# Feed-forward up projections by pairs of m-tiles, in seven block products of 256 tokens

## The chip, the core and the metric

The kernel runs on one core of a Trainium2 chip. The metric is the device time of one execution in microseconds, from the first instruction to the last and what lies around them. Three runs of the kernel before gave 2783.45, 2782.04 and 2782.11 us, median 2782.11. The profile is of one further execution of 2784.78 us.

## What is computed

Two decoder layers on 512 tokens of width 1024, each with a feed-forward, a mixer (a gated delta rule beside attention) and a second feed-forward:

```python
def swiglu(h, w1, w3, w2):
    return (jax.nn.silu(h @ w1) * (h @ w3)) @ w2

for l in range(DEPTH):
    mod = cond @ ada_w[l] + ada_b[l]                 # nine vectors of 1024: shift, scale, gate, three times
    h = modulate(x, norm_ffn1[l], sh1, sc1)
    x = x + 0.5 * (1.0 + g1)[:, None] * swiglu(h, ffn1_w1[l], ffn1_w3[l], ffn1_w2[l])
    h = modulate(x, norm_mix[l], sh2, sc2)
    y = token_mix(h, ...)
    x = x + (1.0 + g2)[:, None] * y
    h = modulate(x, norm_ffn2[l], sh3, sc3)
    x = x + 0.5 * (1.0 + g3)[:, None] * swiglu(h, ffn2_w1[l], ffn2_w3[l], ffn2_w2[l])
```

Everything is float32. w1 and w3 are 1024 x 2816, w2 is 2816 x 1024. The products concerned are h @ w1 and h @ w3 of the four feed-forwards.

## The kernel before

**Number format.** TensorE takes float32r here. Each operand is split into a high part (a copy rounded to float32r, on ScalarE) and a low part (what is left, a subtraction on VectorE), and a product is three matmuls: high by high, high by low, low by high. `mm3` issues them, the weight part being the stationary operand; the activations h lie in `hhi` and `hlo`, features on the 128 partitions, 8 k-tiles of 512 tokens each.

**A slab.** The weights of one m-tile (128 output features) of w1 or w3 are one transfer of 512 KB into a `raw` buffer (2 of them), issued from SyncE (L117). `slab` makes the high part `whi` and the low part `wlo` (3 buffers each) in two halves of 512 columns (L120, L121).

**Up projection.** `up(m)` loads the slabs of w1 and w3 for m-tile m, multiplies each by all 8 k-tiles of h (24 matmuls of 512 columns into a PSUM bank, tags `acc` and `sc`), and `glu` takes SiLU of the one (L443), multiplies it by the other (L444) and splits the result into high and low (L134, L135), which stay in SBUF for the down projection. There are 22 m-tiles.

**Order within a feed-forward.** m-tiles 0 to 8 up, then `down(0)` over the first eight; 9 to 16 up, `down(1)`; 17 to 21 up, `down(2)`. A down projection (`close`) runs over 8 output tiles with slabs of w2. The last one takes four of its tiles in halves of 256 tokens, with the slabs in `A` buffers, so that the next norm can start on one half. The very first feed-forward has had m-tiles 0 to 2 and half of 3 begun during start-up (`begin`, `first_begun`); the others start with `first`, 256 tokens at a time.

**Work between.** The modulation vectors are computed from 512 KB blocks of ada_w, each a transfer into an `L` buffer (5 of them; the conditioning vector `condb` holds one throughout) and one VectorE operation over 1024 columns (L268), pinned behind whatever was traced on VectorE before it. The blocks wait in `self.queue`; `tick(n)` takes n of them, two per m-tile and one per down tile, and `drain` empties the queue before the mixer. A planner orders each engine's instructions otherwise: it issues what its own clock holds ready, earlier lines first, and a tile's buffer is handed on when its last reader has finished.

The only quoted lines that the functions below do not show are the buffer counts:

```python
BUFS = {
    "raw": 2, "wlo": 3, "whi": 3, "hhi": 1, "hlo": 1, "A": 2, "O": 8, "M": 1, "L": 5, "c3": 5, "cv": 3, "g": 7,
    ...
    "ss": 2, "scl": 2, "rk": 2, "acc": 3, "sm": 2, "sc": 2, "po": 1,
}
```

Of the kernel before, what the change touches and what calls it, by code (L numbers as in the profile page):

```python
# [73 lines left out]
class Trunk:  # L74
# [118 lines left out]
    def setup(self):  # L193
# [5 lines left out]
        self.condb = self.t("L", [P, D])  # L199
# [230 lines left out]

    def ffn(self, l, w, gate, finish, early, ahead=None):

        nc = self.nc
        w1, w3, w2 = (self.ap[f"{w}_{n}"] for n in ("w1", "w3", "w2"))
# [5 lines left out]

        def glu(m, ps1, ps3):
# [3 lines left out]
            third = min(m // 8, 2)  # L445
            if third == 1:
                if m == 8:
                    g["hi"] = self.t("A", [P, KT, SEQ], F32R)
                    g["lo"] = self.t("A", [P, KT, SEQ], F32R)
                hi, lo = g["hi"][:, m - 8, :], g["lo"][:, m - 8, :]  # L450
            else:
                o = self.t("O", [P, 2, SEQ], F32R)
                hi, lo = o[:, 0, :], o[:, 1, :]
            self.split(hi, lo, s)
            g[m] = (hi, lo)

        def up(m):
            s1 = up_slab(w1, m)
            s3 = up_slab(w3, m)
            ps1, ps3 = self.p("acc"), self.p("sc")  # L460
            self.proj(ps1, s1, acts)
            self.proj(ps3, s3, acts)
            glu(m, ps1, ps3)
            if m > 2:
                self.tick(2)
# [15 lines left out]
        def first_begun():  # L481
            n = len(early) // 2
            s = up_slab(w3, n)
            for m in range(n):
                glu(m, early[2 * m], early[2 * m + 1])
            ps = self.p("sc")
            self.proj(ps, s, acts)
            glu(n, early[2 * n], ps)
            return n + 1

        def down(i):
# [817 lines left out]
    def run(self, out):  # L1309
# [12 lines left out]
        for l in range(DEPTH):  # L1322
# [21 lines left out]
            self.condb = self.t("L", [P, D])  # L1344
# [34 lines left out]
def layout(inp):  # L1379
# [77 lines left out]
```

## Time and profile before

| | us |
|---|---|
| median of three runs | 2782.11 (2782.04 to 2783.45) |
| profiled execution, device time | 2784.78 |
| its span, first to last instruction | 2782.7 |
| PE busy | 2745.2 (99%) |
| weight loads busy | 2319.4 (83%) |
| VectorE busy | 1703.3 (61%) |
| ScalarE busy | 1087.0 (39%) |
| Pool busy | 192.6 (7%) |
| mean granted TensorE clock | 0.999 |

The feed-forwards lie at about 28 to 392, 1050 to 1400, 1420 to 1760 and 2430 to 2783 us of the span; 87 SiLU operations of line 443 mark them. In what follows a row of groups reads: line, engine, operation, output and inputs by name, shape, count, then busy time and mean nanoseconds of one, then the idle time before it and what ended that. A row of the timeline reads: start, length, engine, line, operation, shape, count. A row of the windows reads: stretch, its length, busy time of PE, of weight loads, VectorE, ScalarE and Pool with counts, granted clock, DMA share, GB/s.

### The profile page before, as it was taken

Reading aid. Unit: us, or ns where it says so; the run is one execution under the profiler, and the core shown is the slowest. Engines: PE = TensorE matmul, PEld = TensorE weight load, DVE = VectorE, ACT = ScalarE, POOL = GpSimd, SP = SyncE. Lnnn points to the kernel's source line nnn. Section 1 sums busy time; section 2 is a strip of 40 time slices with the busy share of each in tenths; the row PEclk is TensorE's granted clock in tenths of the full one; section 3 lists DMA queues with packets and bytes.
Section 4 is the critical chain, followed back from the end, with each engine's and each line's share of the span. In section 5 each row is a group of like instructions: output and inputs, shape, how many; then the busy total and the mean of one; then the engine's idle time right before and its main releaser. Section 6 shows DMA issues by size and latency. Waiting matters only on the chain. (4 is left out here: it accounts for less than half of the span.)

```text
span 2782.7 us, 38556 instructions
## 1 busy us (share of the span) xinstructions
PE 2745.2 (99%) x14648; PEld 2319.4 (83%) x14648; DVE 1703.3 (61%) x3759; ACT 1087.0 (39%) x2301; POOL 192.6 (7%) x312
## 2 busy tenths in 40 slices
PE   7999999999999999999999999999999999999999
PEld 6888888788888888888888888887888888988888
DVE  6555568767668765543455554787767686653333
ACT  4322245544447433232342222545444564332222
POOL 0000015000001010000000000150000111100000
PEclk9999999999999999999999999999999999999999
DMA  7556433222222343643326563333222223443332
GB/s 280 182 184 203 155 103 114 88 73 80 66 78 74 117 159 121 199 143 99 104 93 197 186 203 116 111 100 95 73 80 73 75 73 117 137 137 98 99 99 91
DMA packets 103720, 339.20 MB, mean 122 GB/s; under 512 B 11760, under 2 KB 14448, under 8 KB 103536
## 3 DMA queue, kind: packets, MB, share of 16 engines
q1 hardware_dynamic: 101088, 332.03, 37.7%
q10 hardware_dynamic: 2448, 4.72, 0.4%
q8 instruction: 115, 1.88, 0.3%
q14 instruction: 69, 0.57, 0.1%
HBM read 321.50 MB, written 15.20 MB: 121 GB/s over the span
## 5 line engine op out<-in xcount | busy, mean ns | idle before, releaser
L120 ACT CAST whi<-raw 128x512 fp32r<-128x512 f32 (+1 forms) x834 | 485.3, 610 | 1090.1 <-issue 519.6
L121 DVE TENSOR_TENSOR wlo<-raw,whi 128x512 fp32r<-128x512 f32 (+1 forms) x834 | 571.0, 706 | 258.3 <-ACT whi L120 251.2
L93 PE MATMUL acc<-hhi,whi 128*128 128x512 f32 (+1 forms) x1648 | 645.2, 392 | 7.5 <-DVE cv L522 5.7
L93 PE MATMUL acc<-hlo,whi 128*128 128x512 f32 (+1 forms) x1648 | 626.2, 380 | 1.1 <-POOL hlo L382 0.3
L93 PE MATMUL acc<-hhi,wlo 128*128 128x512 f32 (+1 forms) x1648 | 625.2, 380 | 0.0
L93 PEld LDWEIGHTS acc<-hhi,whi 128*128 128x128 f32 x1648 | 310.7, 189 | 59.8 <-issue 8.2
L93 PEld LDWEIGHTS acc<-hhi,wlo 128*128 128x128 f32 x1648 | 310.9, 189 | 59.1 <-DVE wlo L1284 0.4
L93 PEld LDWEIGHTS acc<-hlo,whi 128*128 128x128 f32 x1648 | 311.9, 189 | 53.0 <-POOL hlo L382 2.9
L93 PE MATMUL acc<-O,whi 128*128 128x512 f32 x1088 | 336.0, 390 | 0.0
L93 PE MATMUL sc<-hhi,whi 128*128 128x512 f32 (+1 forms) x712 | 272.3, 382 | 0.0
L93 PE MATMUL sc<-hhi,wlo 128*128 128x512 f32 (+1 forms) x712 | 272.2, 382 | 0.0
L93 PE MATMUL sc<-hlo,whi 128*128 128x512 f32 (+1 forms) x712 | 271.9, 382 | 0.0
L93 PEld LDWEIGHTS acc<-O,whi 128*128 128x128 f32 x1088 | 203.5, 188 | 41.7
L444 DVE TENSOR_TENSOR g<-g,sc 128x512 f32<-128x512 f32 x87 | 59.8, 688 | 262.8 <-PE sc L93 259.2
L93 PE MATMUL acc<-O,wlo 128*128 128x512 f32 x544 | 211.9, 390 | 0.0
L388 DVE SCALAR_TENSOR_TENSOR M<-acc,gate,M 128x512 f32<-128x512 f32 (+1 forms) x112 | 77.5, 692 | 198.2 <-PE acc L93 191.8
L93 PE MATMUL acc<-A,whi 128*128 128x512 f32 x640 | 197.1, 389 | 0.0
L268 DVE SCALAR_TENSOR_TENSOR L<-L,L 128x1024 f32<-128x1024 f32 x142 | 169.6, 1220 | 0.0
L93 PEld LDWEIGHTS sc<-hhi,wlo 128*128 128x128 f32 x712 | 133.7, 188 | 27.1 <-DVE wlo L121 1.3
L93 PEld LDWEIGHTS sc<-hhi,whi 128*128 128x128 f32 x712 | 134.1, 188 | 26.0
L93 PEld LDWEIGHTS sc<-hlo,whi 128*128 128x128 f32 x712 | 133.9, 188 | 25.8
L93 PEld LDWEIGHTS acc<-A,whi 128*128 128x128 f32 x640 | 120.1, 188 | 25.0
(370 smaller groups left out, 3674.0 us busy)
## 6 DMA issues: line engine op xcount, KB each, us to landing
raw<-in_ffn_w SPq DMA_DIRECT2D x236, 512.0 KB, 3.6
L<-in_ada_w SPq DMA_DIRECT2D x142, 512.0 KB, 4.6
raw<-in_w_in SPq DMA_DIRECT2D x108, 512.0 KB, 3.5
raw<-in_ffn_w SPq DMA_DIRECT2D x32, 384.0 KB, 3.1
raw<-in_w_branch_a SPq DMA_DIRECT2D x16, 512.0 KB, 3.6
raw<-in_w_branch_b SPq DMA_DIRECT2D x16, 512.0 KB, 3.5
raw<-in_w_out SPq DMA_DIRECT2D x16, 512.0 KB, 3.6
spill<-M SPq DMA_DIRECT2D x16, 256.0 KB, 2.0
```

Source lines behind the costliest of these rows:

```text
L93: i = self.nc.tensor.matmul(*a, **k)
L120: nc.scalar.copy(hi[:, s], raw[:, s])
L121: nc.vector.tensor_sub(lo[:, s], raw[:, s], hi[:, s].bitcast(F32))
L268: self.order(self.nc.vector.scalar_tensor_tensor(raw, raw, 1.0, self.condb, ALU.mult, ALU.mult, accum_out=mod[:, o:o + 1]))
L388: self.nc.vector.scalar_tensor_tensor(self.x[:, m, a:b], ps[:, a:b], gate[:, m:m + 1], self.x[:, m, a:b], ALU.mult, ALU.add)
L444: nc.vector.tensor_mul(s, s, ps3)
```

## The change

Two neighbouring m-tiles of both weights are treated as a 2 by 2 block matrix: rows are m-tiles m and m + 1, columns the two halves of the 1024 input features. h is a 2 by 2 block matrix too: halves of the features by halves of the tokens. The four output blocks are made from seven block products in place of eight, Winograd's form of Strassen's scheme. One block product is, for w1 and w3, four k-tiles in three parts: 24 matmuls of 256 columns into one PSUM bank.

- A host-side layout `w13` stores the weights by m-tile and feature half, w1 and w3 together, one 512 KB block each.
- Per pair, `loads` fetches a11, a12 (into `raw`) and a22, and two sums f1 = a21 + a22 and f3 = a21 + a11 (into `L`), each as a transfer from SyncE followed by an adding transfer issued from Pool. `weights` makes f2 = a11 + f1 and f4 = a12 + f2 in place on VectorE. Each of the seven is split into high and low in one operation of 1024 columns on each of ScalarE and VectorE, up to three ahead (`ahead`).
- `fast_acts` makes the four combinations of h once per feed-forward, in the two `A` buffers: eleven VectorE operations over 1024 columns, four copies on ScalarE, three operations on Pool.
- `pairs` runs the seven products per pair. The bank `x` collects products 0, 2, 4 and 6, and ScalarE copies it out after 0, 2 and 4; `z` collects 1 and 5, `y` holds 3. VectorE and once Pool add what is left; SiLU and the gate product work on 256 tokens at a time.
- m-tiles from 6 on (first feed-forward) or from 4 on (the others) are done in pairs; the groups end at 10, 18 and 22. `tick(2)` comes once per pair, no longer once per m-tile, and already from m = 2 for plain tiles.
- The results of m-tiles 8 and 9 go to `c3`, all others to `O`; `condb` moves from `L` to `kph`.

```diff
-        self.condb = self.t("L", [P, D])
+        self.condb = self.t("kph", [P, D])
...
+    def fast_acts(self):
...
+        f32 = lambda t: t.bitcast(F32)
+        b11, b12, b21, b22 = (quarter(i, j) for i in range(2) for j in range(2))
+        store = [self.t("A", [P, 4, 4, 256], F32R) for _ in range(2)]
+        places = [(st[:, i], st[:, i + 1]) for st in store for i in (0, 2)]
...
+        t = difference(b11, b12, nc.vector)
+        split(places[0], t)
+        t3 = difference(b22, b12, nc.gpsimd)
+        minus_sum(t, b22)
+        split(places[1], t)
+        minus_sum(t, b21)
+        split(places[3], t)
+        split(places[2], t3)
+        return [b11, places[0], places[1], b21, places[2], b22, places[3]]
...
-            if m > 2:
+            if m > 1:
                 self.tick(2)
...
+        def block(tag, m, half):
+            t = self.t(tag, [P, 1024])
+            nc.sync.dma_start(t, w13[l, m, half].rearrange("p w k c -> p (w k c)"))
+            return t
+
+        def block_sum(m, half, m2, half2):
+            t = block("L", m, half)
+            nc.gpsimd.dma_start(t, w13[l, m2, half2].rearrange("p w k c -> p (w k c)"), accum_op=ALU.add)
+            return t
+
+        def loads(m):
+
+            st = {}
+            st["f1"] = block_sum(m + 1, 0, m + 1, 1)
+            yield st
+            st["a11"] = block("raw", m, 0)
+            yield st
+            st["f3"] = block_sum(m + 1, 0, m, 0)
+            yield st
+            st["a12"] = block("raw", m, 1)
+            yield st
+            st["a22"] = block("L", m + 1, 1)
+            yield st
+
+        def weights(st):
+
+
+            def parts(t):
+                hi, lo = self.t("whi", [P, 1024], F32R), self.t("wlo", [P, 1024], F32R)
+                nc.scalar.copy(hi, t)
+                nc.vector.tensor_sub(lo, t, hi[:].bitcast(F32))
+                return hi, lo
+
+            yield parts(st["a11"])
+            yield parts(st["f1"])
+            f2, f4 = st["a11"], st["a12"]
+            nc.vector.tensor_add(f2, f2, st["f1"])
+            yield parts(f2)
+            yield parts(f4)
+            nc.vector.tensor_add(f4, f4, f2)
+            yield parts(st["f3"])
+            yield parts(f4)
+            yield parts(st["a22"])
+
+        def product(ps, f, b, fresh):
+
+            for i in range(2):
+                for k in range(4):
+                    c = slice((4 * i + k) * P, (4 * i + k + 1) * P)
+                    x = (b[0][:, k, :], b[1][:, k, :])
+                    self.mm(ps[:, i, :], f[0][:, c], x[0], start=fresh and i == k == 0, stop=False,
+                            skip_group_check=True)
+                    self.mm(ps[:, i, :], f[0][:, c], x[1], start=False, stop=False, skip_group_check=True)
+                    self.mm(ps[:, i, :], f[1][:, c], x[0], start=False, stop=k == 3, skip_group_check=True)
...
+                for step in range(7):
+                    if step in (2, 3, 4, 5, 6):
+                        got = next(nxt, None)
+                        if step == 3 and got is not None:
+                            forms.append(weights(got))
+                    ahead(3)
+                    f = stream.pop(0)
+                    if step == 0:
+                        x = bank("acc")
+                        product(x, f, comb[0], True)
+                        p1 = half("g")
+                        nc.scalar.copy(p1, x)
+                    elif step == 1:
+                        z = bank("sc")
+                        product(z, f, comb[1], True)
+                        p5 = half("cv")
+                        nc.scalar.copy(p5, z)
+                    elif step == 2:
+                        product(x, f, comb[2], False)
+                        u2 = half("g")
+                        nc.scalar.copy(u2, x)
+                    elif step == 3:
+                        y = bank("sm")
+                        product(y, f, comb[3], True)
+                        nc.vector.tensor_add(p1, p1, y)
+                        gated(p1, 0, HALVES[0], None)
+                    elif step == 4:
+                        product(x, f, comb[4], False)
+                        u3 = half("cv")
+                        nc.scalar.copy(u3, x)
+                        nc.gpsimd.tensor_add(p5, p5, u3)
+                    elif step == 5:
+                        product(z, f, comb[5], False)
+                        nc.vector.tensor_add(u2, u2, z)
+                        gated(u2, 0, HALVES[1], None)
+                        gated(p5, 1, HALVES[1], None)
+                        self.split(*place(m), gm[0])
+                    else:
+                        product(x, f, comb[6], False)
+                        s = self.t("cv", [P, 256])
+                        gated(x, 1, HALVES[0], s)
+                        self.split(*place(m + 1), gm[1])
+                self.tick(2)
...
-        for m in range(first_begun() if len(early) > 3 else first(), 9):
-            up(m)
+        begun = len(early) > 3
+        plain = 6 if begun else 4
+        m = first_begun() if begun else first()
+        comb = None
+        while m < plain:
+            up(m)
+            m += 1
+            if comb is None:
+                comb = self.fast_acts()
+        pairs(range(plain, 10, 2), comb)
         down(0)
-        for m in range(9, 17):
-            up(m)
+        pairs(range(10, 18, 2), comb)
         down(1)
-        for m in range(17, FT):
-            up(m)
+        pairs(range(18, FT, 2), comb)
         down(2)
...
+        out[f"{n}_w13"] = A(np.stack([out[f"{n}_{w}"].reshape(L, FT, P, 2, 4, P) for w in ("w1", "w3")], 4)
+                            .transpose(0, 1, 3, 2, 4, 5, 6))
```

More of the change, by code (lines that the diff above doesn't have):

```diff
@@ L439, in up_slab, with place @@
             return self.slab(src[l, m].rearrange("p k c -> p (k c)"), 1024)
+        def place(m):
+            if m in (8, 9):
+                hi, lo = (self.t("c3", [P, SEQ], F32R) for _ in range(2))
+            else:
+                o = self.t("O", [P, 2, SEQ], F32R)
+                hi, lo = o[:, 0, :], o[:, 1, :]
+            g[m] = (hi, lo)
+            return hi, lo
         def glu(m, ps1, ps3):
@@ L444, in glu @@
             nc.vector.tensor_mul(s, s, ps3)
[L445 to L455, printed above, removed]
+            self.split(*place(m), s)
         def up(m):
@@ L489, in first_begun @@
             return n + 1
+        def block(tag, m, half):
[5 more added lines that the diff above has]
+            nc.gpsimd.dma_start(t, w13[l, m2, half2].rearrange("p w k c -> p (w k c)"), accum_op=ALU.add)
+            return t
+        def loads(m):
[10 more added lines that the diff above has]
+            yield st
@@ new lines, in weights @@
+        def weights(st):
[3 more added lines that the diff above has]
+                nc.vector.tensor_sub(lo, t, hi[:].bitcast(F32))
+                return hi, lo
+            yield parts(st["a11"])
[8 more added lines that the diff above has]
+            yield parts(st["a22"])
@@ new lines, in pairs, with ahead, gated @@
+        def pairs(ms, comb):
+            half = lambda tag: self.t(tag, [P, 2, 256])
+            bank = lambda tag: self.p(tag, [P, 2, 256])
+            stream, steps = [], iter(())
+            def ahead(n):
+                while len(stream) < n and forms:
+                    f = next(forms[0], None)
+                    if f is None:
+                        forms.pop(0)
+                    else:
+                        stream.append(f)
+            forms = []
+            for _ in (lds := loads(ms[0])):
+                st = _
+            forms.append(weights(st))
+            ahead(2)
+            for m in ms:
+                nxt = loads(m + 2) if m + 2 in ms else iter(())
+                x, y, z = None, None, None
+                gm = [self.t("g", [P, SEQ]) for _ in range(2)]
+                def gated(q, i, cols, sign):
+                    s = q[:, 0, :] if sign is None else sign
+                    nc.scalar.activation(s, q[:, 0, :], AF.Silu, scale=1.0 if i == 0 else -1.0)
+                    out = gm[i][:, cols[0]:cols[1]]
+                    if i == 0:
+                        nc.vector.tensor_mul(out, s, q[:, 1, :])
+                    else:
+                        nc.vector.scalar_tensor_tensor(out, q[:, 1, :], -1.0, s, ALU.mult, ALU.mult)
+                for step in range(7):
[35 more added lines that the diff above has]
+                        self.split(*place(m), gm[0])
+                    else:
+                        product(x, f, comb[6], False)
[3 more added lines that the diff above has]
+                self.tick(2)
@@ L1343, in run @@
             self.mix(l, vec, self.set_gate(1, mod), done(2, vec, mod), nxt["w"], then(self.ffn_early, l, "ffn2"))
-            self.condb = self.t("L", [P, D])
+            self.condb = self.t("kph", [P, D])
             nc.sync.dma_start(self.condb, self.ap["spill_c"])
```

17 lines of the change are left out of this document (16 added, 1 removed).

## The prediction

> **What bounds the kernel now.** I read the page's first lines, then the chain that ended last, then the tensor engine's own timeline.
>
> ```profile
> span 2782.7 us, 38556 instructions
> PE 2745.2 (99%) x14648; PEld 2319.4 (83%) x14648; DVE 1703.3 (61%) x3759; ACT 1087.0 (39%) x2301; POOL 192.6 (7%) x312
> ...
> 2452.16 5.44 PE acc L93 x24
> 2457.60 5.44 PE sc L93 x24
> ...
> 2517.44 48.96 PE acc L93 x216
> ```
>
> The first line is the span. The second gives each engine's busy time: PE is busy 99% of it, and nothing else comes near. The three others are pieces of the chain: start, length, what. One slab's projection is 24 matmuls in 5.44 us, and the next starts exactly where it ends (2452.16 + 5.44 = 2457.60). So inside a feed-forward PE never waits, and its time is a count times an interval: 5.44 / 24 = 226.7 ns at 512 columns. The change alters the count and the width, so I need the interval at 256 columns. The kernel has such matmuls, in the closing halves and at the start of a feed-forward:
>
> ```profile
> 2762.08 8.80 PE L93 MATMUL acc<-O,A 128*128 128x256 f32 x72
> 2770.71 8.80 PE L93 MATMUL sc<-O,A 128*128 128x256 f32 x72
> ...
> 1420.11 0.28 PE L93 MATMUL acc<-hhi,wlo 128*128 128x256 f32 x1
> ...
> 1421.67 0.28 PE L93 MATMUL acc<-hhi,whi 128*128 128x256 f32 x1
> ...
> 2770.90:2779.50 8.60, 8.60 (x72) 8.41 (x71) 1.94 (x4) 0.00 (x0) 0.00 (x0) 1.00 0.18 61
> ```
>
> 72 matmuls from 2762.08 to 2770.71 are 119.9 ns each, and 13 from 1420.11 to 1421.67 are 120.0 ns. The window row (PE, weight loads, DVE, ACT, POOL) shows why it is not half of 226.7: weight loads fill 8.41 of 8.60 us. Every matmul loads its own 128 columns, so a half-wide matmul has hardly any cover left for its load.
>
> **Matrix work removed and added.** Before, two m-tiles of both weights are 4 slabs x 24 = 96 matmuls at 226.7 ns = 21.76 us. After, 7 products x 2 weights x 4 k-tiles x 3 parts = 168 matmuls at 119.9 ns = 20.14 us. An eighth of the columns goes, but only 1.62 us (7.4%) of the time. Pairs: layer 0's first feed-forward starts them at m = 6, so 8; the three others at m = 4, so 9 each; 35 in all. 35 x 1.62 = **56.7 us** less, if PE never waits. This is the only gain; all that follows can only take from it.
>
> The Trainium skill (TensorE: Matmul & The Clock Gate, Back-to-back issue gap) gives a warm gap of 262 cycles at 256 columns and 518 at 512 and leaves the weight load out. By it a pair would go from 20.7 to 18.3 us, 83 us over all pairs. The 119.9 ns above contradict it at 256, so I keep the rows.
>
> **VectorE and ScalarE inside a pair.** Busy times overlap, so I use start-to-start spacing:
>
> ```profile
> 2465.49 1.22 DVE L268 SCALAR_TENSOR_TENSOR L<-L,L 128x1024 f32<-128x1024 f32 x1
> 2466.64 0.09 DVE L268 DVE_READ_ACCUMULATOR L<-L,L 128x1 f32 x1
> 2466.64 1.22 DVE L268 SCALAR_TENSOR_TENSOR L<-L,L 128x1024 f32<-128x1024 f32 x1
> ...
> 2463.69 1.29 DVE L121 TENSOR_TENSOR wlo<-raw,whi 128x512 fp32r<-128x512 f32 x2
> 2464.89 0.69 DVE L135 TENSOR_TENSOR O<-g,O 128x512 fp32r<-128x512 f32 x1
> ...
> 1402.88 1.26 DVE L378 SCALAR_TENSOR_TENSOR g<-M,gain,po 128x256 f32<-128x256 f32 x3
> 1404.06 1.27 DVE L384 SCALAR_TENSOR_TENSOR hlo<-g,mod,hhi 128x256 fp32r<-128x256 f32 x3
> ...
> 2484.66 1.14 ACT L120 CAST whi<-raw 128x512 fp32r<-128x512 f32 x2 [3.81 <-issue]
> 2485.70 0.62 ACT L134 CAST O<-g 128x512 fp32r<-128x512 f32 x1
> ...
> 1093.53 0.69 DVE L121 TENSOR_TENSOR wlo<-raw,whi 128x512 fp32r<-128x512 f32 x1 [0.32 <-ACT whi L120]
> ```
>
> DVE takes 1.15 us for 1024 columns (2465.49 to 2466.64), 0.60 for 512 (two in 1.20), 0.39 for 256 (three in 1.18); ACT 0.52 for 512. Per pair DVE then has 7 low parts and 2 weight sums of 1024 (9 x 1.15 = 10.35), 2 sums out of PSUM and 2 split subtractions of 512 (2.40), 4 gate products of 256 (1.56) and 2 modulation blocks (2.30): 16.6 us of 20.14, 82%, or 14.3 without the blocks. Before it was 11.8 of 21.76 (8 x 0.60 + 4 x 0.60 + 4 x 1.15). ACT: 7 casts at most 1.04, 4 PSUM copies and 2 split copies of 0.52, 4 SiLU of half width at 0.3 to 0.6, about 12 us. Both fit, so DVE does not bound the average. But does a form come in time?
>
> A form may be made once its slot (3 of whi and wlo) is free, that is when the form three earlier has been multiplied; it is needed two products of 2.88 us later. The crowded place is the end of a pair. Count from the end of step 5: form 2 of the next pair is needed 3 x 2.88 = 8.63 us later. Until then DVE does the PSUM sum 0.60, form 1 1.15, two gate products 0.78, a split 0.60, the sum for form 2 1.15, the last gate product 0.39, a split 0.60, form 2 1.15: 6.4 us; with the two modulation blocks ahead of it, 8.7. Each hand-over from ACT adds some 0.32. So a pair with blocks can miss by nothing or by up to 1.5 us; one without does not. The queue of blocks gives 8 + 6 + 9 + 2 = 25 pairs with blocks (two pops per pair, two per plain tile, 24 in the down projections). Cost 0 to 38 us; I take 0.3 each, **7.5 us**, since the planner issues whatever is ready and three steps seldom all run long.
>
> PSUM reuse is covered: bank x is read by ACT after steps 0, 2 and 4 while a whole other product (2.88 us) runs, against 0.52 for the copy. z has three steps.
>
> **Pool.** One 512-wide addition per pair, and the issue of two adding transfers.
>
> ```profile
> L1210 POOL TENSOR_TENSOR g<-g,M 128x512 f32<-128x512 f32 x16 | 26.2, 1640 | 163.3 <-DVE g L1209 159.5 <-DMA raw<-in_w_branch_b 3.8
> L614 POOL TENSOR_TENSOR g<-g,const 128x512 f32<-128x512 f32 x16 | 23.3, 1454 | 46.9 <-DVE kap L627 34.3 <-issue 7.0 <-DVE sc L625 5.4
> ```
>
> It takes 1.5 to 1.6 us and starts about 0.6 after step 4; its reader is due 2.88 after that step, so it costs nothing unless an adding transfer, which waits on Pool for the landing of its first half, holds it up by over 0.7. The Trainium skill (SBUF — State Buffer, Who interferes with whom) says that a DVE instruction with two SBUF inputs contends with a GpSimd instruction that reads SBUF. By it DVE could lose up to 1.6 us more per pair, 18.2 of 20.14; no row here separates it, and it would only make the DVE rival below likelier.
>
> **Transfers.** Per pair before: 4 weight blocks of 512 KB and 4 modulation blocks. After: 5 plain, 2 adding and 2 modulation blocks.
>
> ```profile
> core 0: us, PE busy (x) PEld busy (x) DVE busy (x) ACT busy (x) POOL busy (x), PEclk, DMA share, GB/s
> 28.00:392.00 364.00, 363.17 (x1664) 303.40 (x1664) 220.12 (x397) 112.36 (x209) 0.00 (x0) 1.00 0.58 184
> ...
> raw<-in_ffn_w SPq DMA_DIRECT2D x236, 512.0 KB, 3.6
> ...
> A<-in_ffn_w SPq DMA_DIRECT2D x4, 512.0 KB, 8.6
> ```
>
> 184 GB/s at a share of 0.58 is 317 GB/s, so a plain block costs the engines 1.65 us; one lands 3.6 us after issue, 8.6 in the crowded start. The trace has no adding transfer. It can't cost less than a plain one (1.65); the crowded row bounds it at 8.6. With c times a plain block, a pair with modulation blocks needs 11.6 + 3.3 c us of the engines against 20.14: nothing is late up to c = 2.6. I take c = 2, nearer the lower end, since two streams of 512 KB have to be brought together. The two chains (load, then add) are then some 3.6 + 7 us, and the slots of L let them start about a pair (20 us) ahead: hidden, cost **0**.
>
> **Once per feed-forward.** fast_acts adds 11 DVE operations of 1024 (12.7 us), 4 copies on ACT and 3 on Pool, hidden under the plain tiles (two are 21.8 us, DVE free 40% by the window above) and the work before them; only places[0] is due at the first pair's second product. 0 to 4 us in all, I take 1.5. Fewer pops leave 4 modulation blocks and the rope tables (layer 0) and 2 blocks (layer 1) for the drain ahead of the mixer: 6 x 1.15 plus some 4 us of small operations on DVE, which there is
>
> ```profile
> 392.00:440.00 48.00, 46.67 (x303) 41.52 (x304) 34.94 (x92) 29.16 (x61) 15.36 (x16) 1.00 0.19 61
> ```
>
> 73% busy beside a PE at 97%: 0 to 11, I take 3. The second A buffer is free for the last down projection's spare slabs only after the last product, but they are wanted 4 x 4.08 = 16 us later: 0. Eleven joints between pairs and down projections, 0 to 1 us each: 3.
>
> **Sum.** The profiled execution took 2784.8 us (span 2782.7 and 2.1 around it). 2784.8 - 56.7 + 7.5 + 1.5 + 3 + 3 = 2743.1. The runs' median, 2782.1, lies 2.7 below the profiled one, so **2740 us**. All bounds at their best give 2725, all at their worst (38 + 4 + 11 + 11 = 64) 2790; the likely part of that is 2725 to 2758.
>
> **Rivals.**
> - *DVE late in the pairs* (chance 0.17). For it: 82% busy, in order, waits on ACT and PE between. Against: three forms of stock. At 1.5 us in 25 pairs instead of 0.3: 30 us more, 2770.
> - *The adding transfers become the bound* (0.17; the slower side). Place: the 16 DMA engines in the pairs with modulation blocks. It decides from c = 2.6; gain and loss are even at c = 3.3 (25 x 2.28 us = 57). At c = 4 such a pair needs 24.8 us and one without 21.5: 25 x 4.7 + 10 x 1.3 = 130, so 2870. For it: nothing in the trace adds in a transfer, and the share is already 0.58. Against: the down projections let the queue recover, and c = 4 is 6.6 us, not far below the crowded row's 8.6.
> - *The change does not do what it says* (0.05): products with their own waits and three operand tiles run at 125 rather than 119.9 ns. 35 x 0.86 = 30 us more, 2770; even at 129.5 ns (21.76 / 168).
> - *The weight load hides better than in the rows* (0.03): the interval falls to half of that at 512, 113.35 ns, because two matmuls in a row hold the same high part: 35 x 168 x 6.55 ns = 39 us less, 2701. Against: the closing halves have the same order and show 119.9. The gap of the page named above would go further, to some 109 ns.
>
> **Chances.** The forecast holds 0.58. No change to within 0.2% is 2776.5 to 2787.7 (a measurement here cannot tell less). Faster: 0.58, the last rival 0.03, and of the second side most of DVE late (0.11) and of the slow products (0.03) = 0.75. Same: 0.05. Slower: mostly the transfers, 0.20. The range reaches from 2718, just below the best sum, to 2800, past the worst; it leaves out most of the transfer rival and the last one. The likeliest case alone is 2725 to 2758.
>
> **What would show it.** Right: products of 24 matmuls at 2.88 us, back to back; PE near 99%; weight loads over 90% of PE in the pairs; DVE about 80% there; Pool's additions under 2 us. Wrong: idle time before the first matmul of a product, released by DVE's low part (DVE late) or by ACT's cast of a block that has only just landed (transfers); adding blocks that land over 4.3 us (c = 2.6) apart; an interval other than 119.9 ns.

## The result, and the profile after

The changed kernel took 2799.73 us (median of four runs, 2798.02 to 2803.0) against 2782.38 (2782.04 to 2783.45) for the kernel before: 1.0063 times as long, 95% interval 1.0046 to 1.0081. 2740 was predicted; slower had a chance of 0.20.

From the page of the changed kernel: span, busy times, and the engines' shares of the chain of waits.

```profile
span 2796.3 us, 44477 instructions
PE 2711.5 (97%) x17168; PEld 2406.5 (86%) x17168; DVE 2048.5 (73%) x3978; ACT 1288.0 (46%) x2494; POOL 350.3 (13%) x429
...
PE 74%; DVE 14%; DMA 5%; ACT 3%; issue 2%; POOL 2%; SPq 0%; ACTq 0%; DVEq 0%; POOLq 0%
```

PE is busy for 34 us less than before in a span that is 14 us longer. It now waits, and DVE holds 14% of the chain. Did the products do what they should? Timeline of PE in the last group of layer 1's first feed-forward, then the window over that group (PE, weight loads, DVE, ACT, Pool, clock, DMA share, GB/s):

```profile
1709.85 0.40 PE L93 MATMUL acc<-A,whi 128*128 128x256 f32 x2
1710.09 0.28 PE L93 MATMUL acc<-A,wlo 128*128 128x256 f32 x1
1710.21 0.40 PE L93 MATMUL acc<-A,whi 128*128 128x256 f32 x2
...
1703.00:1743.00 40.00, 40.00 (x336) 40.00 (x335) 32.16 (x39) 22.23 (x34) 4.80 (x4) 1.00 0.65 199
```

Three matmuls from 1709.85 to 1710.21 are 120 ns each, on new operands too, and PE never stops. DVE is at 80%, as predicted. So the 56.7 us are there. What took them is seen by cutting PE's timeline at the first matmul of each stage: the length of a stage, less its count times 226.7 or 119.9 ns for groups and plain tiles, or less the kernel before for the rest. "Starts" are plain tiles, the second feed-forwards' closings with the next start, and the mixers from their long run of 252 matmuls on; "closings" run from the first matmul of down(2) of a first feed-forward to that long run (layer 0: 350.10 to 483.69 us).

| us lost | starts | groups of pairs | closings (layer 0, 1) | sum |
|---|---|---|---|---|
| changed kernel | 38.0 | 10.8 | 22.2 (133.6, 126.5; before 118.6, 119.3) | 71.0 |

71.0 - 56.7 = 14.3; the spans differ by 13.6. So three places, and the largest is the start.

**The start.** Layer 0's second feed-forward in the changed kernel, timelines of DVE, Pool, ACT and PE:

```profile
1062.16 3.42 DVE L448 TENSOR_TENSOR L<-L,hlo 128x1024 f32<-128x1024 f32 x1
1065.68 1.56 DVE L449 TENSOR_TENSOR L<-L,hlo 128x1024 f32<-128x1024 f32 x1
...
1070.56 3.26 DVE L454 SCALAR_TENSOR_TENSOR L<-L,hhi 128x1024 f32<-128x1024 f32 x1
...
1061.91 2.58 POOL L447 TENSOR_TENSOR L<-hhi 128x1024 f32<-128x1024 f32 x1
...
1066.23 3.21 POOL L448 TENSOR_TENSOR L<-L,hlo 128x1024 f32<-128x1024 f32 x1
1069.52 3.22 POOL L449 TENSOR_TENSOR L<-L,hlo 128x1024 f32<-128x1024 f32 x1
...
1067.27 1.04 ACT L458 CAST A<-L 128x1024 fp32r<-128x1024 f32 x1 [5.63 <-DVE L L449]
1068.34 1.28 ACT L492 ACT_TABLE_LOAD   x1
...
1070.12 1.13 ACT L120 CAST whi<-raw 128x512 fp32r<-128x512 f32 x2
...
1070.79 0.80 PE L93 MATMUL sc<-hhi,whi 128*128 128x512 f32 x1 [3.36 <-ACT whi L120]
...
1075.08 0.79 PE L93 MATMUL sc<-hhi,wlo 128*128 128x512 f32 x1 [3.07 <-DVE wlo L121]
```

The combinations of h are ready to run as soon as the norm has written h, and they stand ahead of the first tiles' own work. Some of them are also stretched by operations of Pool. DVE and Pool in the very first start:

```profile
59.74 1.21 DVE L448 TENSOR_TENSOR L<-L,hlo 128x1024 f32<-128x1024 f32 x1
60.99 3.30 DVE L449 TENSOR_TENSOR L<-L,hlo 128x1024 f32<-128x1024 f32 x1
...
59.97 3.24 POOL L448 TENSOR_TENSOR L<-L,hlo 128x1024 f32<-128x1024 f32 x1 [0.69 <-DVE hlo L1444]
```

DVE's L448 begins before Pool's operation and takes 1.21 us though Pool runs beside it. L449 begins while Pool's operation runs, and ends at 64.29, 1.08 us after Pool's end at 63.21. L448 at 1062.16 and L454 at 1070.56 do the same: the one ends 1.09 us after Pool's L447, the other 1.08 after its L449. Of the 44 DVE operations of the combinations, 16 began during one of Pool's and each ended 1.08 to 1.09 us after it; the other 28 took 1.21 to 1.23 us. So an operation that begins during Pool's is held until Pool's is over. That makes the 16 together 18.1 us longer; in the start shown above it is 5.6 us.

The rest is the order. ACT stands 5.63 us in order behind DVE's L449 with a cast for the combinations, and only then loads the SiLU table and casts the weights (L120), for which PE waits 3.36; then DVE's low part, 3.07. Windows of the changed kernel, and of the kernel before:

```profile
1070.00:1080.00 10.00, 6.15 (x14) 4.37 (x15) 9.97 (x11) 5.64 (x10) 2.74 (x1) 0.51 0.30 91
1080.00:1090.00 10.00, 10.00 (x45) 8.21 (x44) 7.40 (x10) 4.23 (x8) 0.00 (x0) 0.98 0.35 121
```

```profile
1070.00:1080.00 10.00, 10.00 (x46) 8.29 (x45) 3.86 (x7) 3.40 (x6) 0.00 (x0) 1.00 0.56 172
```

14 matmuls in 10 us instead of 46, and the granted clock is 0.51: the waits are paid twice. The clock was at half for 10.2 us from 1070.14, which is before the first of the two waits was over (1070.79). Over the span the mean clock is 0.991, before 0.999; 0.008 x 2796 = 22 us at most of the 71 are the slower clock, at most because PE waited for a part of that time.

**The closing.** DVE and PE in layer 0's first feed-forward, changed kernel, then DVE before:

```profile
381.86 1.28 DVE L121 TENSOR_TENSOR wlo<-raw,whi 128x512 fp32r<-128x512 f32 x2
383.06 1.22 DVE L268 SCALAR_TENSOR_TENSOR L<-L,kph 128x1024 f32<-128x1024 f32 x1
...
386.49 1.22 DVE L268 SCALAR_TENSOR_TENSOR L<-L,kph 128x1024 f32<-128x1024 f32 x1
...
387.98 0.15 DVE L349 TENSOR_SCALAR nv<-sm 128x2 f32<-128x2 f32 x1
...
388.57 4.21 PE L93 MATMUL sc<-O,A 128*128 128x256 f32 x18 [3.75 <-DVE M L388]
```

```profile
386.74 0.42 DVE L323 TENSOR_TENSOR g<-g,g 128x256 f32<-128x256 f32 x1 [0.54 <-ACT g L322]
387.08 0.15 DVE L349 TENSOR_SCALAR nv<-sm 128x2 f32<-128x2 f32 x1
```

Four modulation blocks stand from 383.06 to 387.64 in front of the norm's chain (L349) and of the residual for which PE waits. In the kernel before the queue was empty by then. Up to the mixer's first matmul the closings took 44.7 and 42.6 us, before 34.7 and 34.8: 17.8 of the 22.2 us are lost there.

**Transfers.** Queues (packets, MB, share of the engines) and issues (count, KB, us to landing) of the changed kernel:

```profile
q1 hardware_dynamic: 106128, 350.38, 37.7%
q0 software_dynamic: 10080, 36.70, 7.4%
...
raw<-in_ffn_w SPq DMA_DIRECT2D x166, 512.0 KB, 4.5
...
L<-in_ffn_w POOLq DMA_DIRECT2D x70, 512.0 KB, 7.6
```

Per MB an adding block costs (7.4 / 36.70) / (37.7 / 350.38) = 1.87 times a plain one, and it lands 7.6 us after issue.

**The groups.** 7.1 of their 10.8 us are in one group, at the first pair of layer 1's first feed-forward. PE and ACT there:

```profile
1470.14 0.50 PE L93 MATMUL sc<-A,whi 128*128 128x256 f32 x2 [1.03 <-ACT whi L560]
...
1488.88 0.50 PE L93 MATMUL acc<-A,whi 128*128 128x256 f32 x2 [2.73 <-ACT cv L647]
...
1487.29 1.04 ACT L560 CAST whi<-raw 128x1024 fp32r<-128x1024 f32 x1 [5.38 <-DMA raw<-in_ffn_w]
1488.24 0.58 ACT L647 COPY cv<-acc 128x512 f32<-128x512 f32 x1
```

PE waits for form 1, the sum f1, first for its high part and then for its low part. Then it waits 2.73 us in front of the seventh product: ACT's copy of the bank (L647) stands in order behind a cast for the next pair, and that cast waits for its block to land. The smaller losses of the other groups are this second wait too.

### The profile page after: what moved, and what is told of

Its sections match the earlier page's. It is cut to its first block, busy times and chain, and to the rows that moved or that the text cites. A ratio compares the mean times of both kernels' runs of the same rounds, so it can differ in the third digit from the quotient of the medians.

```text
span 2796.3 us, 44477 instructions
## 1 busy us (share of the span) xinstructions
PE 2711.5 (97%) x17168; PEld 2406.5 (86%) x17168; DVE 2048.5 (73%) x3978; ACT 1288.0 (46%) x2494; POOL 350.3 (13%) x429
## 3 DMA queue, kind: packets, MB, share of 16 engines
q1 hardware_dynamic: 106128, 350.38, 37.7%
q0 software_dynamic: 10080, 36.70, 7.4%
## 4 chain that ended last, share of the span: by engine, by line
PE 74%; DVE 14%; DMA 5%; ACT 3%; issue 2%; POOL 2%; SPq 0%; ACTq 0%; DVEq 0%; POOLq 0%
PE acc L93 52%; PE sc L93 14%; PE sm L93 4%; DMA raw<-in_ffn_w 3%; DVE wlo L121 2%; PE sm L98 2%; DVE L L268 1%; PE po L93 1%; DVE cv L699 1%; ACT whi L120 1%; DVE g L378 1%; DVE L L831 1%; DVE L L833 1%; DVE hlo L384 1%; DMA raw<-in_w_in 0%
## 5 line engine op out<-in xcount | busy, mean ns | idle before, releaser
L120 ACT CAST whi<-raw 128x512 fp32r<-128x512 f32 (+2 forms) x554 | 320.8, 606 | 400.1 <-PE acc L93 309.2
L93 PE MATMUL acc<-hlo,whi 128*128 128x512 f32 (+1 forms) x1368 | 487.2, 356 | 4.9 <-POOL hlo L382 3.9
L121 DVE TENSOR_TENSOR wlo<-raw,whi 128x512 fp32r<-128x512 f32 (+2 forms) x554 | 395.9, 732 | 76.7 <-ACT whi L120 69.4
L93 PE MATMUL acc<-A,whi 128*128 128x256 f32 (+1 forms) x1808 | 348.3, 292 | 4.7 <-ACT cv L647 4.7
L93 PEld LDWEIGHTS acc<-A,whi 128*128 128x128 f32 x1808 | 287.0, 192 | 11.0 <-ACT cv L647 5.7
L93 PEld LDWEIGHTS acc<-hhi,whi 128*128 128x128 f32 x1368 | 259.3, 190 | 42.6 <-issue 10.1
L93 PE MATMUL acc<-A,wlo 128*128 128x256 f32 (+1 forms) x904 | 263.3, 291 | 0.0
L561 DVE TENSOR_TENSOR wlo<-raw,whi 128x1024 fp32r<-128x1024 f32 x140 | 171.0, 1222 | 92.0 <-ACT whi L560 87.3
L560 ACT CAST whi<-raw 128x1024 fp32r<-128x1024 f32 x140 | 146.5, 1047 | 190.9 <-PE acc L93 101.7
L93 PEld LDWEIGHTS acc<-A,wlo 128*128 128x128 f32 x904 | 173.9, 192 | 2.5
L268 DVE SCALAR_TENSOR_TENSOR L<-L,kph 128x1024 f32<-128x1024 f32 x142 | 171.0, 1227 | 0.0
```

Of the source, the lines that this page charges most:

```text
L93: i = self.nc.tensor.matmul(*a, **k)
L120: nc.scalar.copy(hi[:, s], raw[:, s])
L121: nc.vector.tensor_sub(lo[:, s], raw[:, s], hi[:, s].bitcast(F32))
L268: self.order(self.nc.vector.scalar_tensor_tensor(raw, raw, 1.0, self.condb, ALU.mult, ALU.mult, accum_out=mod[:, o:o + 1]))
L560: nc.scalar.copy(hi, t)
L561: nc.vector.tensor_sub(lo, t, hi[:].bitcast(F32))
```

## The experiments

My theory: the starts' loss is the combinations, the closings' is the left-over modulation blocks, and both are places in an engine's order and not its total time. The rival: VectorE (or the adding transfers) simply has no room, and whatever is moved only moves the wait. Edits are to the changed kernel unless another is named. All ledgers are from one profiled execution each, as in the table above; they agree with the spans to within 2 us.

### The two causes, one at a time

**no_combinations**: plain quarters of h take the combinations' places in the products, so the up projections are not the reference's.

```diff
+    def no_acts(self):
...
+        return [b11, b12, b22, b21, b12, b22, b11]
...
-                comb = self.fast_acts()
+                comb = self.no_acts()
```

> Leaves out the making of the four combinations of h (the products use plain quarters of h in their place, so the output is another); all products, transfers and weight sums stay. Theory (the combinations stand on VectorE, ScalarE and Pool in front of what the second half of the first tiles needs): the starts lose 11.5, 9.9, 11.8 and 6.3 us against the kernel before, about 39; nearly all of it comes back, 2760 us, and the second feed-forward's tile 1 (the 512-wide matmul after the 256-wide ones) waits under 0.5 us. Rival (the pairs' extra load or the adding transfers slow the starts): under 10 us come back, 2790 or more.

2760.61 us, 0.9915 (0.9898 to 0.9931). Starts lose 0.1 in place of 38.0, closings 24.4, groups 9.7. The time falls by 39.1 us and the starts' ledger by 37.9: the starts' loss is the combinations'. The closings' is not.

**ticks_earlier**: in `close`, two blocks per tile in the first two down projections.

```diff
-            self.tick()
+            self.tick(1 if spare else 2)
```

> Two modulation blocks per tile in the first two down projections instead of one, so that the queue is empty before the last down projection. Theory (blocks that used to be done earlier now stand in front of the closing norm's chain): the closings of the two first feed-forwards, 44.7 and 42.6 us from the last pair to the mixer's first matmul against 34.7 and 34.8, go back to about 35, and the mixer's start of layer 0 gains up to 5: 2799.7 - 18 to 23 = 2777 to 2782. Rival (the late A buffer delays the spare slabs): the closings keep 5 us or more each, 2788 or more.

2818.57, 1.0126 (1.0107 to 1.0144): a miss. The closings did return, 119.9 and 119.6, but the groups lost 57.0. SP, ACT and PE at the group after the first down projection, in this run:

```profile
179.42 17.03 SPq L533 DMA_DIRECT2D L<-in_ffn_w  x4
...
193.07 1.05 ACT L560 CAST whi<-L 128x1024 fp32r<-128x1024 f32 x1 [15.90 <-DMA L<-in_ffn_w]
...
194.17 0.79 PE L93 MATMUL sc<-A,whi 128*128 128x256 f32 x2 [4.11 <-ACT whi L560]
```

PE waits for form 1, whose two transfers must follow each other. SP's queue spends 17 us on four issues into L. The extra blocks use the same five buffers: of SP's waits from 175 to 200 us, 17.0 were for modulation blocks (L268) to give one back, the longest 10.9; in the changed kernel it is 12.9 in the same stretch, the longest 5.1.

### Moving the combinations

**no_pool_share**:

```diff
-        t3 = difference(b22, b12, nc.gpsimd)
+        t3 = difference(b22, b12, nc.vector)
```

> The third combination's three operations on VectorE in place of Pool, nothing else. Theory A (VectorE and Pool slow each other: VectorE's operations took 3.4 us where 1.2 is usual while Pool's ran): VectorE's total at the starts falls or stays, every one of these operations is back at 1.2 us, the starts gain 3 to 6 us each, about 2783. Theory B (only the place in the order counts): VectorE has 3.5 us more to do at the same place, the starts get 1 to 3 us worse each, about 2807.

2792.13, 1.0033 (1.002 to 1.0046), between the times of the two theories. Starts lose 1.3 in place of 38.0. DVE in layer 0's second feed-forward:

```profile
1063.87 1.76 DVE L448 TENSOR_TENSOR L<-L,hlo 128x1024 f32<-128x1024 f32 x1
...
1067.82 0.68 DVE L121 TENSOR_TENSOR wlo<-raw,whi 128x512 fp32r<-128x512 f32 x1
```

L448 takes 1.76 us in place of 3.42. But the planner's order changed as well: the tile's first low part now stands behind four combination operations, at 1067.82, where the changed kernel had it behind five, at 1074.34. So this run does not say how much of the starts' loss was Pool's hold and how much the order. The groups lose 42.0, 37.4 of it in the first group of each feed-forward:

```profile
1095.35 0.86 POOL L538 DMA_DIRECT2D L<-in_ffn_w  x1 [1.44 <-DMA L<-in_ffn_w]
...
1099.99 1.04 ACT L560 CAST whi<-L 128x1024 fp32r<-128x1024 f32 x1 [9.21 <-DMA L<-in_ffn_w]
```

ACT waits 9.21 us for form 1's landing. The late start had hidden how late form 1 is. The wait in front of the seventh product is there too, in the same pairs.

**combinations_pinned**: all 18 operations kept in program order, like this one.

```diff
-            eng.tensor_sub(t, f32(a[0]), f32(b[0]))
+            self.order(eng.tensor_sub(t, f32(a[0]), f32(b[0])))
```

> Each operation of the combinations is pinned behind what was traced before it on its engine, so behind tile m = 2 (4 in the first feed-forward); the same work on the same engines. Theory (the planner let them float ahead into the norm and the first tiles): the starts gain most of their 39 us, what remains is up to 3 us each where the first pair waits for its second operand: 2762 to 2775. Rival (the work itself is too much wherever it stands): the loss moves to the first pairs and the time stays within 8 us of 2799.7.

2818.58, 1.0127 (1.0112 to 1.0142), slower than either side had it. Starts 3.7, groups 61.0: the loss moves to the first pairs (13.4 to 16.3 us each) and grows. Pinned, the combinations stand on VectorE behind the modulation blocks, and they still hold L.

Is it the buffers L that form 1 waits for? Two tests, both with the combinations on VectorE alone:

**combinations_in_c3**:

```diff
-        new = lambda: self.t("L", [P, 4, 256])
...
+            ts = [self.t("c3", [P, 2, 256]) for _ in range(2)]
```

> The four differences of h are made on VectorE alone, and their two working tiles are taken as halves of 512 from the buffers c3, which lie idle then, in place of two of the five buffers L; the operations are twice as many at half the width. To be set against no_pool_share (2792.1 us), whose first groups of pairs lost 7.6, 8.8, 11.1 and 9.9 us waiting for the first pair's f1. Theory: f1 is late because its buffer L is held by the differences and the modulation blocks, and its two transfers start only when one comes free; with L left alone the first groups lose 0 to 2 us each as in no_combinations, and the time is 2757 to 2766 us. Rival: VectorE itself is late (18 us of combinations ahead of the first pair's parts and of places[0]); then the first groups lose as much as before and the time is 2788 to 2796 us.

2786.07, 1.0013 (1.0004 to 1.0022). The groups fall from 42.0 to 5.5, as the theory had it; but the starts lose 27.6 again, and the time is not the one expected. DVE and ACT:

```profile
1077.07 1.28 DVE L459 TENSOR_TENSOR c<-c,hlo 128x512 f32<-128x512 f32 x2
...
1083.57 2.49 DVE L121 TENSOR_TENSOR wlo<-raw,whi 128x512 fp32r<-128x512 f32 x4
...
1075.01 1.14 ACT L120 CAST whi<-raw 128x512 fp32r<-128x512 f32 x2
```

ACT has cast a slab of the last plain tile at 1075; DVE makes its low part at 1083.57, behind the combinations, whose working tiles are now in c3, and behind two modulation blocks.

**one_more_L**: no_pool_share with other buffer counts.

The buffer counts that differ:

```diff
-    ... "L": 5, ... "g": 7,
-    "s1": 6, ...
+    ... "L": 6, ... "g": 6,
+    "s1": 5, ...
```

> no_pool_share with six buffers L in place of five (and six of g in place of seven, five of s1 in place of six, to make room). If buffers L are what f1 waits for, one more takes at least half of the 37 us that the first groups lose: 2760 to 2776 us. If VectorE is what is late: 2788 to 2796 us. If the g taken away is needed by the pairs, a loss at every pair shows: over 2800 us.

2777.12, 0.9978 (0.9969 to 0.9988): just above the window given. Groups 27.1 in place of 42.0, starts 0.7. The first groups lose 12.8 in place of 37.4 and wait for form 1 no more, as with c3; what is left are waits in front of a seventh product, and they come in the second groups too. It supports the same reading, with the reservation that g and s1 changed too.

**combinations_spread**: combinations_in_c3, every operation in `self.order`, in four parts; `next(making)` comes after each of the last two plain tiles and in steps 0 and 1 of the first pair.

```diff
+        def parts():
+            t = difference(b11, b12)
+            split(places[0], t)
+            yield
+            minus_sum(t, b22)
+            split(places[1], t)
+            yield
+            split(places[2], difference(b22, b12))
+            yield
+            minus_sum(t, b21)
+            split(places[3], t)
+            yield
```

> combinations_in_c3 (2786.1 us), with the differences kept in program order in four parts: one after each of the last two plain tiles, one in each of the first two steps of the first pair. There the first groups were right (0 to 1.7 us) and the last plain tile waited 4.7 us and ran on at half clock, because VectorE made all the differences ahead of that tile's weight parts. Theory: spread out, the plain tiles lose under 1 us and the first groups under 2: 2756 to 2765 us. Rival, after combinations_pinned: VectorE has not the room in the first pair either, and the first groups lose 5 us or more each: 2780 to 2800 us.

2802.35, 1.0068 (1.0053 to 1.0083): the rival's side. Starts 2.1, groups 49.5. DVE:

```profile
1093.52 1.22 DVE L268 SCALAR_TENSOR_TENSOR L<-L,kph 128x1024 f32<-128x1024 f32 x1
...
1094.67 0.69 DVE L449 TENSOR_TENSOR c<-hhi 128x512 f32<-128x512 f32 x1
```

The first combination comes at 1094.67, after the modulation blocks behind which it is pinned, when the first pair is due; before that DVE had idle time. So this run did not show that the room is missing, only that it was not used.

**combinations_in_turn**: combinations_spread with no operation in `self.order`; part 1 after the last plain tile but one, parts 2 and 3 after the last, part 4 in step 1.

```diff
             split(places[1], t)
-            yield
             split(places[2], difference(b22, b12))
...
-                    if step in (0, 1):
+                    if step == 1:
                         next(making, None)
```

> combinations_in_c3 (2786.1 us) with the differences given out in three parts and left free to be placed: the first after the second last plain tile, the next two after the last plain tile, the last in the first pair's second step. On VectorE the last plain tile's weight parts then stand ahead of the later differences, and no difference stands behind the modulation blocks as it did in combinations_spread. Theory: VectorE has room for the 18 us of differences where they don't stand in front of a plain tile's weight parts or behind held blocks; starts and first groups together lose under 3 us per feed-forward: 2756 to 2768 us. Rival: the time of VectorE before the first pairs is simply spent, and the wait moves once more: 2780 us or more.

2768.24, 0.9938 (0.9922 to 0.9955). Starts 4.8, groups 15.6 (of it 8.1 in one group of layer 0). The same VectorE work in another order costs 18 us less than in c3 and 34 less than spread. The room is there; the place in the order decides. The time is 0.24 us above the window given.

### The modulation blocks and the adding transfers

**no_adding_transfers**: the sums f1 and f3 lack their second block.

```diff
-            nc.gpsimd.dma_start(t, w13[l, m2, half2].rearrange("p w k c -> p (w k c)"), accum_op=ALU.add)
```

> The changed kernel with the second transfer of each sum f1 and f3 left out (so the weight sums lack one block; all else is the same). Theory: the adding transfers, at about 1.9 times a plain block's engine time, are hidden but for the joint of layer 1's first feed-forward (7 us) and a few us at the other joints: 2783 to 2795 us. Rival (the adding transfers set the end): 2770 us or less. If they cost nothing at all: 2797 to 2803 us.

2787.01, 1.0014 (1.0005 to 1.0024): 12.7 us less, as the theory had it. Groups 1.1 in place of 10.8, all else as it was. The adding transfers do not set the end, but they cost about 10 us: at a joint form 1 comes late, and inside the pairs the next pair's block lands late, so that ACT's cast of it holds up the bank's copy.

**c3_and_three_ticks**: combinations_in_c3, and after each pair

```diff
-                self.tick(2)
+                self.tick(3)
```

> combinations_in_c3, and three modulation blocks after each pair in place of two: 47 of the 49 blocks are popped before the last down projection in place of 38. Theory: the two closings of the layers' first feed-forwards return from 132.5 and 127.8 us (down(2) to the mixer) to 120 each, as they did in ticks_earlier, and the pairs bear a third block: 16 to 20 us less than combinations_in_c3. Rival, after ticks_earlier: the blocks' hold on L makes f1 and f3 late at the pairs and takes it all back: 0 to 20 us more than combinations_in_c3.

2786.9, 1.0015 (1.0006 to 1.0024), no gain on c3: closings 7.0 in place of 22.2, groups 27.5 in place of 5.5. The rival holds. ACT at the second pair after the first down projection, and issues in 1585 to 1632:

```profile
1626.57 1.04 ACT L566 CAST whi<-raw 128x1024 fp32r<-128x1024 f32 x1 [7.98 <-DMA raw<-in_ffn_w]
```

```profile
raw<-in_ffn_w SPq DMA_DIRECT2D x4, 512.0 KB, 9.3
```

There the blocks' transfers and the pair's run in one burst, and a weight block lands 9.3 us after issue, not 4.5. The cast that waits for it stands in front of the bank's copy, and PE waits for its seventh product.

**blocks_after_norm**, in `close`:

```diff
-            self.tick()
+            if finish is None:
+                self.tick()
...
-        self.tick(len(ws))
```

> The changed kernel, with no modulation block worked off in the last down projection; what is left of the queue runs after its closing norm, ahead of the mixer (what it holds is wanted only at the mixer's end). Theory: the two slow closings were eight blocks standing on VectorE in front of the norm; they return to about 120 us from 133.6 and 126.5 (down(2) to the mixer), the mixer's start hides the blocks, and the pairs are untouched: 2779 to 2785 us. Rival: the blocks make the mixer's start late by as much: 2792 to 2802 us.

2801.62, 1.0066 (1.0051 to 1.0081): the rival. The norm chain is free, but PE waits at the mixer's start. PE and DVE:

```profile
419.00 0.76 PE L93 MATMUL acc<-hhi,whi 128*128 128x512 f32 x1 [8.87 <-DVE cv L699]
...
414.35 1.23 DVE L268 SCALAR_TENSOR_TENSOR L<-L,kph 128x1024 f32<-128x1024 f32 x1
...
415.50 0.74 DVE L699 SCALAR_TENSOR_TENSOR cv<-acc,vec,cv 128x509 f32<-128x509 f32 x1
```

The convolution (L699) that frees PE's bank stands on DVE behind the left-over blocks.

**no_combinations_blocks_after_norm** and **spread_and_blocks_after_norm** join this edit with those two kernels.

> no_combinations (2760.6 us; plain quarters of h, the differences left out, so what is computed is not the reference's) with the modulation blocks after the closing norm. It is the sum that was predicted, with the two terms that were mis-sized taken out on the chip: 2738 to 2745 us by the theory. If something else holds a part of the 59 us between the prediction and the result, it stays above 2750 us.

2764.39, 0.9931 (0.9914 to 0.9947): a miss; closings 28.9, starts 0.2. It does not test the sum, since that cure is none.

> Both of the above edits. If the two losses are separate and both are cured: 2738 to 2748 us, about the time that was predicted for the change. If either only moves: 2760 to 2785 us.

2810.88, 1.01 (1.0085 to 1.0115), above both windows: the two losses add up, groups 52.2 and closings 32.8.

**in_turn_and_chosen_ticks**: combinations_in_turn, and after each pair

```diff
-                self.tick(2)
+                self.tick(2 if m in (10, 12) else 3)
```

> combinations_in_turn, with three modulation blocks after a pair in place of two, but for the two pairs behind the first down projection, which were the ones that waited in c3_and_three_ticks: 45 of the 49 blocks are popped before the last down projection in place of 38. Theory: the closings take 122 to 126 us (132 and 128 in combinations_in_c3) and no group loses over 3 us more: 6 to 14 us less than combinations_in_turn. Rival: the queue of transfers is full in the other pairs too, and what the closings give the groups take: within 4 us of combinations_in_turn or above it.

2754.09, 0.9897 (0.9882 to 0.9911), 14.2 less than in_turn: the theory. This version beats both kernels. Span, and the window of a start:

```profile
span 2748.7 us, 44559 instructions
```

```profile
1059.00:1087.00 28.00, 27.31 (x120) 22.29 (x120) 27.01 (x43) 15.39 (x25) 0.88 (x1) 1.00 0.46 134
```

DVE is busy for 27.01 of 28.00 us in the start, and PE hardly waits. Starts 2.7, groups 9.0, closings 12.1 (129.2 and 120.8), 23.8 in all. The closings gain less than the 122 to 126 each that were expected. The groups lost less as well (9.0 against 15.6), nearly all of it in one group, where a wait in front of the seventh product is 1.70 us in place of 5.45; why the block landed earlier there is open. The ledgers' difference is above that of the times, and the profiled execution of in_turn was the slowest of its runs, that of this kernel the fastest.

**rope_tables_earlier**, on top of it:

```diff
-                self.tick(2 if m in (10, 12) else 3)
+                self.tick(2 if m in (10, 12) else 4 if m == 20 else 3)
...
-            if l == 0:
-                self.queue.append(self.rope_tables)
+                if l == 0 and j == 5:
+                    self.queue.append(self.rope_tables)
```

> in_turn_and_chosen_ticks (2754.1 us) with the rotary tables put after the fourth chunk of modulation blocks in the queue in place of at its end, and a fourth block after the last pair. Its closing in layer 0 still took 129.2 us against 118.6 in the kernel before: two modulation blocks and the tables stand on VectorE in front of the norm chain there. Theory: with one or two of them gone the closing takes 120 to 124 us: 2745 to 2750 us. Rival: the tables and the further block cost the pairs as much: 2752 to 2760 us.

2755.94, 0.9907 (0.989 to 0.9923): no change against the run before it. That is the time that the rival gave, but its mechanism did not come: the groups lost no more, about 8 us. Layer 0's closing is still 127.9; what its last 9 us are is open.

## Why the prediction was wrong

- **Matrix work, -56.7.** Right. 119.9 to 120 ns in the new products, and the ledger closes with it: 71.0 lost, 56.7 gained, 13.6 measured. The rivals with slower products or better hidden weight loads fall. So does the gap of 262 cycles at 256 columns that the Trainium skill gives (TensorE: Matmul & The Clock Gate, Back-to-back issue gap).
- **Once per feed-forward, 1.5 (0 to 4).** This is the step that failed: 38 us. It said "hidden under the plain tiles" and compared totals. VectorE has the room in total (in_turn_and_chosen_ticks: 2.7 us), but what counts is who stands behind the new work in each engine's order. The planner placed it as soon as h is there, in front of the first tiles' weight parts, with ACT in line behind DVE. In c3, with no share on Pool, the combinations still cost the starts 27.6 us.

The second part of this step is Pool. The prediction gave it no price beside fast_acts, and there its operations held 16 of the 44 DVE operations, 18.1 us in all. How the 38 us divide between the two no run separates. The Trainium skill (SBUF — State Buffer, Who interferes with whom) says that a DVE instruction with two SBUF inputs contends with a GpSimd instruction that reads SBUF. The trace agrees: such an operation, begun during Pool's, took up to 3.42 us in place of 1.21. The prediction asked this only of the pairs and found that no row separates it. Rows of the kernel before do, DVE and Pool (L1210, the row that it had quoted):

```profile
956.41 2.39 DVE L121 TENSOR_TENSOR wlo<-raw,whi 128x512 fp32r<-128x512 f32 x2
...
956.58 1.68 POOL L1210 TENSOR_TENSOR g<-g,M 128x512 f32<-128x512 f32 x1 [55.02 <-DVE g L1209]
```

Two low parts take 2.39 us where two take 1.29 elsewhere, and the second ends 0.54 us after Pool's operation. In the pairs it happened as well: in 23 of the 35 DVE's sum f2 (L567) began beside Pool's addition and took some 2.2 us in place of 1.22. There it costs PE next to nothing, for without adding transfers the groups lose 1.1 us in all.

- **Fewer pops, the drain, 3 (0 to 11).** Failed as well: 22.2. It put the left-over blocks into the drain ahead of the mixer. But down(2) takes eight pops of its own, which found an empty queue before and find blocks now, in front of the norm chain. 17.8 us are lost ahead of the mixer's first matmul; the 4.4 us behind it are within what the prediction allowed for the drain. ticks_earlier and in_turn_and_chosen_ticks show that this loss follows the queue. The late A buffers are not it: the last feed-forward's closing, with equally late buffers, took 33.6 us from its first matmul to the start of its last, against 33.5.
- **DVE late in the pairs, 7.5 (0 to 38).** Right within its range, too high: with the adding transfers left out the groups lose 1.1 in all.
- **Adding transfers, 0.** The price was right (c = 1.87 for 2), so the rival with this bound falls. The Trainium skill (Collectives: The Full Stack, The bandwidth ceiling) says of a collective, ReduceScatter, that its addition needs two source reads per chunk where the copy of AllGather needs one, with a measured ratio of 1.93. The 1.87 here lies near it, but this is no collective, and no run here shows the reason. Hidden they were not everywhere: without them the groups lose 9.7 us less.
- **"PSUM reuse is covered", 0.** Not so: the prediction set 0.52 us for ACT's copy against a product of 2.88, and left out that ACT works in order. Before the seventh product the copy stood behind a cast that waited for a block, 2.73 us of PE at 1488.88 and smaller waits in the other groups. It is also what the groups lose in one_more_L and in c3_and_three_ticks.
- **Joints, 3 (0 to 11).** Right in its bounds. Most of the groups' 10.8 us are in a first pair, but there the wait before the seventh product is larger than the two for form 1 (1.03 and 0.83 us).
- **Sum and range.** Losses of 15 were predicted, 71 came. 2799.73 lies at the edge of the range (2718 to 2800), for a reason that was on no list of rivals; "slower" stood on the wrong mechanism.
- **What would show it wrong** named low parts and casts late in front of a product. They are what PE waits for in the plain tiles, and once in a pair (1470.14 and the matmul at 1471.47).

## What to carry to other kernels

When new work is called hidden, write down what stands behind it on each engine it touches, at the place where a planner will put it (as soon as its inputs are there), and not the engine's free share. Over the kernel without combinations (2760.6), the combinations cost 39 us as they were and 58 pinned, both with a share on Pool; on VectorE alone 32 in L, 25 in other buffers, 42 spread behind the blocks and 8 given out in turn. Ask also which operations of two engines hold each other up. A shared queue that was always empty at some point is a property worth checking: with fewer places to work it off, its rest lands in the most exposed stretch. And a buffer taken for a short while can delay a chain of two transfers that has to start early.

## What the runs showed of the hardware

- A VectorE operation with two operands in SBUF that begins during one of Pool's was over 1.08 us after Pool's at 1024 columns (16 of 16 in the combinations), and some 0.55 after it at 512 (24 low parts of the kernel before). One that began before Pool's was not held (1.21 us at 59.74).
- The granted clock was at half for 10.2 us around two PE waits of 3.36 and 3.07 us, from 0.65 us before the first was over. In one_more_L a single wait of 2.66 us, over at 1130.09, came with 3.4 us at half from 1129.87. The Trainium skill (TensorE: Matmul & The Clock Gate, What's actually happening) puts half rate behind at least one idle window of about 3.4 us. The runs agree in kind, but these waits were shorter, and there the measurement decides.
- An adding transfer took 1.87 times the engine time of a plain one per MB, and 7.6 us to land against 4.5.
